# Shift and scale of attention in one adaLN block: a different split of the column sums between VectorE, ScalarE, GpSimd and TensorE

## The chip, the core and the metric

The kernel runs on one core of one Trainium2 chip. The metric is the device time of one execution in microseconds; the time given for a kernel is the median of several executions.

## The reference

One transformer block with adaptive layer norm, sequence 512, width 2048, all in float32. A conditioning vector `c` makes six vectors of 2048 numbers, and the first two of them, a shift and a scale, are applied to the normed input before one wide projection. Only this front part is touched by the change:

```python
sh_a, sc_a, g_a, sh_f, sc_f, g_f = jnp.split(jax.nn.silu(c) @ ada_w[l] + ada_b[l], 6, axis=-1)
h = rms_norm(x, norm_mix[l]) * (1.0 + sc_a[:, None, :]) + sh_a[:, None, :]
proj = h @ w_in[l]          # 2048 x 5656: convolution gates, q, k, v and gate logits
...                         # convolution mixer and sparse attention, out projection
x = x + g_a[:, None, :] * (y @ w_out[l])
h = modulate(rms_norm(x, norm_ffn[l]), sh_f, sc_f)
x = x + g_f[:, None, :] * ((jax.nn.silu(h @ ffn_w1[l]) * (h @ ffn_w3[l])) @ ffn_w2[l])
```

`ada_w` is 2048 x 12288. Shift and scale of attention are its first 4096 columns, 33.5 MB.

## The kernel before, in words

The kernel works through stages one after the other: the start stage (this change), the rest of q, k and v together with the compression of k and v, attention woven with the convolutions, the out projection, and the feed-forward part. Every product with a weight is done as three fp32r matmuls (`mm3`, L98 to L100) on operands split into a high and a low part; `load_split` (L85) loads a weight tile `raw` on SyncE's queue, casts the high part `whi` on ScalarE (L92) and subtracts on VectorE for the low part `wlo` (L93).

The **start stage** makes the input columns in steps. A column here is one block of 128 of the 2048 features, `k` from 0 to 15. Before the steps, x is loaded (4 MB), the row norms are taken, and four diagonal matrices `dg` are made from them (L270); TensorE turns x and scales it at once with 64 matmuls against `dg` (L278), which gives `xnT`, all 16 columns.

A step (`STEP = 2` columns, so eight steps) then has two parts, and `weave` puts the instructions of one part between those of the other, with 1.3 pieces of side work for each piece of main work:

- **side work** (`start_steps`): shift and scale of the *next* two columns. For scale and for shift apart (`m` = 1, 0), 256 columns of `ada_w` are loaded on SyncE's queue, four pieces of 512 KB, `ada_w` being laid so that each partition holds 16 rows. The 16 rows times `silu(c)` are added up per partition: 10 rows on VectorE (L187, L189), and 6 rows (`SHARE`) by ScalarE multiplying (L183) and GpSimd adding (L185); L192 adds the two sums. `ada_cols` then turns the sum `acc` on TensorE (L206) and VectorE sums over partitions (L208), which leaves 128 numbers per column in `shf` and `gsc`.
- **main work** (`start_columns`): `h` is `xnT` times scale plus shift on ScalarE (L293), split into `ahi` (L295) and `alo` (L296), and multiplied with `w_in`: 512 columns for k and v into `main` (24 matmuls), 128 for the gate logits (6), and, at fixed columns, 512 each for `ksv` and `q` in `aux`, which VectorE adds into SBUF (L322). All told 39 matmuls of 512 moving columns for each of the 16 columns, 624 in the stage. The first of a step needs `alo`, and with it shift and scale.

Each engine runs its instructions in the order in which they were put in its queue, so an instruction that waits holds what stands behind it on the same engine. The order printed below is that queue order.

Of the kernel before, what the change touches and what calls it, by code (L numbers as in the profile page):

```python
# [17 lines left out]
P = 128  # L18
D = 2048
S = 512  # L20
# [49 lines left out]
def block_kernel(ctx: ExitStack, tc: tile.TileContext, a: dict, out: bass.AP):  # L70
# [95 lines left out]
    def ada_steps(ring, width, c0, n, bias=False, second=None, share=0):  # L166


        acc = accp.tile([P, 512], F32, tag="acc", name="acc")[:, :n]
        acc2 = second.tile([P, 512], F32, tag="acc2", name="acc2", bufs=2)[:, :n] if share else None  # L170
        step = min(width // n, KC)
        yield acc
        if bias:
            nc.gpsimd.memset(acc, 0.0)
            nc.sync.dma_start(acc[0:1, :], a["ada_b"][:, c0:c0 + n])
        for k0 in range(0, KC, step):
            raw = ring.tile([P, width], F32, tag="araw", name="araw")
            rv = raw[:, :step * n].rearrange("p (k n) -> p k n", k=step)
            nc.sync.dma_start(rv, ada_v[:, k0:k0 + step, c0:c0 + n])
            for k in range(k0, k0 + step):  # L180
                w, s = rv[:, k - k0, :], cT[:, k:k + 1]
                if k < share:
                    nc.scalar.activation(w if k else acc2, w, AF.Copy, scale=s)  # L183
                    if k:
                        nc.gpsimd.tensor_add(acc2, acc2, w)  # L185
                elif k == share and not bias:
                    nc.vector.tensor_scalar(acc, w, s, None, op0=ALU.mult)  # L187
                else:
                    nc.vector.scalar_tensor_tensor(acc, w, s, acc, op0=ALU.mult, op1=ALU.add)  # L189
            yield  # L190
        if share:
            nc.vector.tensor_add(acc, acc, acc2)  # L192

    def ada(*args, **kw):
        steps = ada_steps(*args, **kw)
        acc = next(steps)
        for _ in steps:
            pass
        return acc
# [31 lines left out]
    aring = pool("araw", 4, stack=st0)  # L231
    STEP, AW, SHARE = 2, 1024, 6

    def start_steps(k0):

        if k0 < KC:
            for m in (1, 0):
                steps = ada_steps(aring, AW, m * D + k0 * P, STEP * P, second=sp, share=SHARE)
                acc = next(steps)
                yield from steps  # L240
                ada_cols(aux, acc, 0, m, k0, STEP)

    first = start_steps(0)
# [28 lines left out]
    for _ in range(KC * STEP * P // AW):  # L272
        next(first)
    xnT = []
    for k in range(KC):
        ps = aux()
        for i in range(NT):
            nc.tensor.matmul(ps[:, i * P:(i + 1) * P], xts[i][:, k * P:(k + 1) * P], dgs[i], start=True, stop=True)  # L278
        t = act.tile([P, S], F32, tag="alo", name="xnT")
        (nc.vector.tensor_copy if k % 4 == 3 else nc.scalar.copy)(t, ps)  # L280
        xnT.append(t)

# [3 lines left out]
    for _ in first:  # L286
        pass

    def start_columns(k0):
        n = STEP  # L290
# [17 lines left out]
        for c0, dst, ends in ((CKS, ksv, (0, 2, 4, 8, 12, 16)), (CQ, q0, (0, 2, 6, 10, 14, 16))):  # L308
# [3 lines left out]
            ws = [load_split(ring, rows(w_in, k, 2, c0, 512), 2, 512) for k in ks[::2]]  # L312
            for i in range(NT):
                ps = aux()
                tok = slice(i * P, (i + 1) * P)
                for k in ks:
                    mm3(ps, [h[:, tok] for h in hT[k]], [t[:, k % 2, :] for t in ws[(k - ks[0]) // 2]],
                        k == ks[0], k == ks[-1])
# [6 lines left out]
    for k0 in range(0, KC, STEP):  # L325
        weave(start_columns(k0), start_steps(k0 + STEP), 1.3)
# [834 lines left out]
```

## Time and profile before

| | |
|---|---|
| median of 3 runs | 2291.96 us (2291.7 to 2303.21) |
| the profiled execution | 2294.12 us, its span 2292.4 us |
| TensorE busy | 2220.5 us, 97% of the span |
| VectorE busy | 1684.2 us, 73% |
| ScalarE busy | 958.6 us, 42% |
| GpSimd busy | 132.0 us, 6% |
| start stage, first matmul with weights to the last | 44.57 to 219 us |

The times of single instructions come from one profiled execution. Busy times of TensorE overlap (matmuls are pipelined), so the time from the start of one matmul to the start of the next tells what one costs, not its duration. A row with two numbers of matmul records for one matmul is a plain fp32 matmul, which leaves two records; an fp32r matmul leaves one.

### The profile page before, as it was taken

How to read it: one execution, taken by the hardware profiler on the slowest of the kernel's cores; microseconds unless marked ns; L12 is line 12 of the kernel's file. 1: busy time of each engine (PE TensorE's matmuls, PEld its weight loads, DVE VectorE, ACT ScalarE, POOL GpSimd, SP SyncE). 2: the span in 40 equal slices, each digit the busy share in tenths (PEclk: the TensorE clock that was granted, in tenths of full speed). 3: DMA queues.
4: the chain of work that ended last, by engine and by line, in shares of the span. 5: the costliest groups of instructions: out<-in, count | busy, mean ns of one | idle time of the engine just before them, and what ended most of it. 6: DMA issues, size and time to landing. Idle time of an engine off the chain costs nothing.

```text
span 2292.4 us, 30011 instructions
## 1 busy us (share of the span) xinstructions
PE 2220.5 (97%) x11223; PEld 1856.7 (81%) x11223; DVE 1684.2 (73%) x2569; ACT 958.6 (42%) x1598; POOL 132.0 (6%) x205
## 2 busy tenths in 40 slices
PE   5889999999999999999999999999999999999999
PEld 4667777778787777788888888888888788888887
DVE  6996857877856773988888888888888655533356
ACT  6544434555444223744444444444444432222221
POOL 2430000000000000000000000000000200000010
PEclk9999999999999999999999999999999999999999
DMA  8785555545534873264333444434442675533243
GB/s 292 257 272 155 168 177 172 170 135 150 148 99 148 297 266 111 88 188 125 120 120 119 121 120 124 124 117 122 124 121 74 233 236 196 175 106 124 96 153 115
DMA packets 374406, 358.60 MB, mean 156 GB/s; under 512 B 14856, under 2 KB 288620, under 8 KB 373236
## 3 DMA queue, kind: packets, MB, share of 16 engines
q1 hardware_dynamic: 365364, 325.22, 45.3%
q0 software_dynamic: 8896, 31.46, 4.0%
q8 instruction: 88, 1.44, 0.3%
q14 instruction: 58, 0.48, 0.1%
HBM read 336.70 MB, written 19.92 MB: 156 GB/s over the span
## 4 chain that ended last, share of the span: by engine, by line
PE 45%; issue 36%; DVE 9%; DMA 7%; ACT 2%; POOL 1%; SPq 0%; POOLq 0%; DVEq 0%; ACTq 0%
PE main L98 8%; PE main L100 8%; PE main L99 8%; DMA araw<-in_ada_w 5%; DVE acc L189 4%; PE aux L98 4%; PE aux L100 4%; PE aux L99 4%; PE aux L676 2%; PE aux L648 1%; DVE wlo L93 1%; DMA raw<-in_w_in 1%; POOL gd L916 1%; PE aux L864 1%; PE main L864 1%
## 5 line engine op out<-in xcount | busy, mean ns | idle before, releaser
L92 ACT CAST whi<-raw 128x1024 fp32r<-128x1024 f32 (+1 forms) x168 | 171.6, 1021 | 464.9 <-PE main L100 268.6
L93 DVE TENSOR_TENSOR wlo<-raw,whi 128x1024 fp32r<-128x1024 f32 (+1 forms) x168 | 200.4, 1193 | 219.7 <-ACT whi L92 218.9
L864 PE MATMUL main<-hC,whi 128*128 128x512 f32 x1408 | 355.9, 394 | 5.5 <-DVE hC L881 3.3
L857 DVE TENSOR_TENSOR wlo<-raw,whi 128x1024 fp32r<-128x1024 f32 x218 | 265.8, 1220 | 107.4 <-ACT whi L852 107.4
L852 ACT CAST whi<-raw 128x1024 fp32r<-128x1024 f32 x218 | 228.2, 1047 | 259.3 <-PE main L864 129.1
L189 DVE SCALAR_TENSOR_TENSOR acc<-araw,cT,acc 128x512 f32<-128x512 f32 (+1 forms) x392 | 270.8, 692 | 79.0 <-DMA araw<-in_ada_w 69.2
L864 PEld LDWEIGHTS main<-hC,whi 128*128 128x128 f32 x1408 | 254.3, 190 | 52.1 <-DVE hC L881 4.4
L864 PE MATMUL aux<-hC,whi 128*128 128x512 f32 x1072 | 269.6, 393 | 0.0
L864 PEld LDWEIGHTS aux<-hC,whi 128*128 128x128 f32 x1072 | 193.7, 190 | 34.8
L866 PEld LDWEIGHTS main<-hC,wlo 128*128 128x128 f32 x1408 | 192.9, 191 | 13.9
L866 PE MATMUL main<-hC,wlo 128*128 128x256 f32 x1408 | 197.1, 283 | 0.0
L98 PE MATMUL main<-alo,whi 128*128 128x512 f32 x448 | 181.2, 405 | 11.3 <-DVE alo L296 11.3
L99 PE MATMUL main<-ahi,wlo 128*128 128x512 f32 x448 | 177.4, 396 | 0.0
L100 PE MATMUL main<-ahi,whi 128*128 128x512 f32 x448 | 177.1, 395 | 0.0
L866 PEld LDWEIGHTS aux<-hC,wlo 128*128 128x128 f32 x1072 | 146.4, 190 | 10.5
L98 PE MATMUL main<-wlo,ahi 128*128 128x512 f32 x384 | 152.1, 396 | 0.1
L100 PE MATMUL main<-whi,ahi 128*128 128x512 f32 x384 | 150.8, 393 | 0.0
L99 PE MATMUL main<-whi,alo 128*128 128x512 f32 x384 | 150.6, 392 | 0.0
L866 PE MATMUL aux<-hC,wlo 128*128 128x256 f32 x1072 | 149.8, 282 | 0.0
L852 ACT CAST whi<-t 128x1024 fp32r<-128x1024 f32 x84 | 88.3, 1051 | 136.5 <-PE aux L864 70.9
L98 PE MATMUL main<-wlo,ghi 128*128 128x512 f32 x352 | 138.3, 394 | 3.4 <-ACT ghi L1086 2.7
L98 PE MATMUL aux<-wlo,ghi 128*128 128x512 f32 x352 | 137.8, 391 | 0.0
(278 smaller groups left out, 3821.2 us busy)
## 6 DMA issues: line engine op xcount, KB each, us to landing
raw<-in_ffn_w SPq DMA_DIRECT2D x264, 512.0 KB
araw<-in_ada_w SPq DMA_DIRECT2D x136, 512.0 KB
araw<-in_ada_w SPq DMA_DIRECT2D x112, 256.0 KB
raw<-in_w_in SPq DMA_DIRECT2D x128, 192.0 KB
raw<-in_w_in SPq DMA_DIRECT2D x40, 512.0 KB
raw<-in_w_out SPq DMA_DIRECT2D x32, 512.0 KB
gd<-d POOLq DMA_DIRECT2D x44, 256.0 KB, 2.3
graw<-gd POOLq DMA_DIRECT2D x44, 256.0 KB, 4.2
```

The lines of the kernel that those rows point to most:

```text
L92: nc.scalar.copy(hi[:, :m], raw[:, :m])
L93: nc.vector.tensor_sub(lo[:, :m], raw[:, :m], hi[:, :m].bitcast(F32))
L98: nc.tensor.matmul(ps, lhs[0], rhs[1], start=first, stop=False)
L99: nc.tensor.matmul(ps, lhs[1], rhs[0], start=False, stop=False)
L100: nc.tensor.matmul(ps, lhs[0], rhs[0], start=False, stop=last)
L189: nc.vector.scalar_tensor_tensor(acc, w, s, acc, op0=ALU.mult, op1=ALU.add)
L648: nc.tensor.matmul(one[b], queries(g, i, h), kT[b][g][:, :L], start=True, stop=True)
L676: nc.tensor.matmul(po[:, b * HD:(b + 1) * HD], s["pT"][b][:, kb * P:(kb + 1) * P], vv[b][:, kb, g * HD:(g + 1) * HD], start=kb == 0, stop= ...
L852: nc.scalar.copy(hi, t)
L857: nc.vector.tensor_sub(lo, t, hi.bitcast(F32))
L864: nc.tensor.matmul(ps, wt[0][:, ks[k]], hC[p][:, k, :], start=first and k == 0, stop=False, skip_group_check=True)
L866: nc.tensor.matmul(ps[:, HS:], wt[1][:, ks[k]], hC[p][:, k, 0:HS], start=False, stop=last and k == HK - 1, skip_group_check=True)
```

## The change

- **Sums.** Shift and scale of a step are loaded side by side in one tile (`raw`, four `k` rows of 512 columns). VectorE adds up three of the four tiles (12 rows, L246 and L248 of the changed kernel) over both at once. The last tile goes to TensorE with the sum `acc`: for each block of 128 columns, `j`, 5 matmuls into partitions `32 j` to `32 j + 31` of one PSUM tile, with `crep` (`silu(c)` copied 32 times) or ones as the stationary operand of 32 columns (L254). ScalarE copies the result (`asb`, L258), one small matmul against a strided identity (L259) turns it, and VectorE adds the bias (L263) and makes the scale (L266). The shares of ScalarE and GpSimd (L183, L185, L192), the turns L206 and the sums L208 are gone.
- **Loads.** These loads are issued by GpSimd's queue (L241) in place of SyncE's, from a ring of three tiles of 1 MB in place of four of 512 KB.
- **x turned per step.** The matmuls against `dg` (L229 now) stand in `start_steps`, for the step's columns alone; all copies of `xnT` are ScalarE's.
- **Steps.** The first two steps have one column each (`PLAN`), then seven of two; the weave ratio is 0.7, and the blocks of `ksv` and `q` have an additional end after one column.

```diff
--- before.py
+++ after.py
@@ -163,13 +163,10 @@

     ada_v = ada_w.rearrange("(p k) n -> p k n", k=KC)

-    def ada_steps(ring, width, c0, n, bias=False, second=None, share=0):
+    def ada(ring, width, c0, n, bias=False):

         acc = accp.tile([P, 512], F32, tag="acc", name="acc")[:, :n]
-        acc2 = second.tile([P, 512], F32, tag="acc2", name="acc2", bufs=2)[:, :n] if share else None
         step = min(width // n, KC)
-        yield acc
         if bias:
             nc.gpsimd.memset(acc, 0.0)
             nc.sync.dma_start(acc[0:1, :], a["ada_b"][:, c0:c0 + n])
@@ -179,23 +176,10 @@
             nc.sync.dma_start(rv, ada_v[:, k0:k0 + step, c0:c0 + n])
             for k in range(k0, k0 + step):
                 w, s = rv[:, k - k0, :], cT[:, k:k + 1]
-                if k < share:
-                    nc.scalar.activation(w if k else acc2, w, AF.Copy, scale=s)
-                    if k:
-                        nc.gpsimd.tensor_add(acc2, acc2, w)
-                elif k == share and not bias:
+                if k == 0 and not bias:
                     nc.vector.tensor_scalar(acc, w, s, None, op0=ALU.mult)
                 else:
                     nc.vector.scalar_tensor_tensor(acc, w, s, acc, op0=ALU.mult, op1=ALU.add)
-            yield
-        if share:
-            nc.vector.tensor_add(acc, acc, acc2)
-    def ada(*args, **kw):
-        steps = ada_steps(*args, **kw)
-        acc = next(steps)
-        for _ in steps:
-            pass
         return acc

     def ada_cols(psum_tile, acc, which, m, k0, n):
@@ -228,19 +212,59 @@
     ksv = kp.tile([P, NT, 512], F32, name="ksv")
     q0 = kp.tile([P, NT, 512], F32, name="q0")
     raw_kv = kp.tile([P, 2, NKV, S], F32, name="raw_kv")
-    aring = pool("araw", 4, stack=st0)
-    STEP, AW, SHARE = 2, 1024, 6
-    def start_steps(k0):
-        if k0 < KC:
-            for m in (1, 0):
-                steps = ada_steps(aring, AW, m * D + k0 * P, STEP * P, second=sp, share=SHARE)
-                acc = next(steps)
-                yield from steps
-                ada_cols(aux, acc, 0, m, k0, STEP)
-    first = start_steps(0)
+    aring = pool("araw", 3, stack=st0)
+    PLAN = [(0, 1), (1, 1)] + [(k, 2) for k in range(2, KC, 2)]
+    AK = 4
+    crep = sp.tile([P, KC, 32], F32, name="crep")
+    nc.vector.tensor_copy(crep, cT[:, :, None].to_broadcast([P, KC, 32]))
+    xnT = []
+    def start_steps(k0, cn):
+        for k in range(k0, k0 + cn):
+            ps = aux()
+            for i in range(NT):
+                nc.tensor.matmul(ps[:, i * P:(i + 1) * P], xts[i][:, k * P:(k + 1) * P], dgs[i], start=True, stop=True)
+            t = act.tile([P, S], F32, tag="alo", name="xnT")
+            nc.scalar.copy(t, ps)
+            xnT.append(t)
+            yield
+        an, nq = cn * P, 2 * cn
+        acc = accp.tile([P, 512], F32, tag="acc", name="acc")[:, :nq * P]
+        raws = []
+        for k in range(0, KC, AK):
+            raw = aring.tile([P, AK, 512], F32, tag="araw", name="araw")
+            for m in range(2):
+                c0 = m * D + k0 * P
+                nc.gpsimd.dma_start(raw[:, :, m * an:(m + 1) * an], ada_v[:, k:k + AK, c0:c0 + an])
+            if k + AK < KC:
+                for kk in range(AK):
+                    w, s = raw[:, kk, :nq * P], cT[:, k + kk:k + kk + 1]
+                    if k + kk == 0:
+                        nc.vector.tensor_scalar(acc, w, s, None, op0=ALU.mult)
+                    else:
+                        nc.vector.scalar_tensor_tensor(acc, w, s, acc, op0=ALU.mult, op1=ALU.add)
+                yield
+        ps = aux()
+        for kk in range(AK + 1):
+            lhs, w = (crep[:, k + kk, :], raw[:, kk, :]) if kk < AK else (ones[:, 0:32], acc)
+            for j in range(nq):
+                nc.tensor.matmul(ps[32 * j:32 * j + 32, :P], lhs, w[:, j * P:(j + 1) * P], start=kk == 0, stop=kk == AK,
+                                 skip_group_check=True)
+        m = 32 * nq
+        asb = sp.tile([P, P], F32, tag="asb", name="asb", bufs=2)
+        nc.scalar.copy(asb[:m], ps[:m, :P])
+        nc.tensor.matmul(ps[:, 256:256 + nq], asb[:m], ident[:m, 0:m:32], start=True, stop=True, skip_group_check=True)
+        yield
+        for m, d in ((1, gsc), (0, shf)):
+            d = d[:, 0, k0:k0 + cn]
+            nc.vector.tensor_add(d, ps[:, 256 + m * cn:256 + (m + 1) * cn], bcol[:, m * KC + k0:m * KC + k0 + cn])
+            if m:
+                g0 = at["norm_mix"] + k0
+                nc.vector.scalar_tensor_tensor(d, d, 1.0, cols[:, g0:g0 + cn], op0=ALU.add, op1=ALU.mult)
     vrow = sp.tile([nrow, P], F32, name="vrow")
     brow = sp.tile([NB6, P], F32, name="brow")
     at, r0 = {}, 0
@@ -269,25 +293,13 @@
         dg = sp.tile([P, P], F32, name=f"dg{i}")
         nc.vector.tensor_scalar(dg, ident, ss, None, op0=ALU.mult)
         dgs.append(dg)
-    for _ in range(KC * STEP * P // AW):
-        next(first)
-    xnT = []
-    for k in range(KC):
-        ps = aux()
-        for i in range(NT):
-            nc.tensor.matmul(ps[:, i * P:(i + 1) * P], xts[i][:, k * P:(k + 1) * P], dgs[i], start=True, stop=True)
-        t = act.tile([P, S], F32, tag="alo", name="xnT")
-        (nc.vector.tensor_copy if k % 4 == 3 else nc.scalar.copy)(t, ps)
-        xnT.append(t)
     hT = []
     ps_kv = [main() for _ in range(4)]
     ps_gl = aux()
-    for _ in first:
+    for _ in start_steps(*PLAN[0]):
         pass

-    def start_columns(k0):
-        n = STEP
+    def start_columns(k0, n):
         for k in range(k0, k0 + n):
             h = sp.tile([P, S], F32, tag="h", name="h", bufs=2)
             nc.scalar.activation(h, xnT[k], AF.Identity, scale=gsc[:, 0, k:k + 1], bias=shf[:, 0, k:k + 1])
@@ -305,16 +317,17 @@
             mm3(ps_gl, [t[:, kk, :] for t in w], hT[k0 + kk], k0 + kk == 0, k0 + kk == KC - 1)
         yield

-        for c0, dst, ends in ((CKS, ksv, (0, 2, 4, 8, 12, 16)), (CQ, q0, (0, 2, 6, 10, 14, 16))):
+        for c0, dst, ends in ((CKS, ksv, (0, 1, 2, 4, 8, 12, 16)), (CQ, q0, (0, 1, 2, 6, 10, 14, 16))):
             if k0 + n not in ends:
                 continue
             ks = range(ends[ends.index(k0 + n) - 1], k0 + n)
-            ws = [load_split(ring, rows(w_in, k, 2, c0, 512), 2, 512) for k in ks[::2]]
+            m = min(len(ks), 2)
+            ws = [load_split(ring, rows(w_in, k, m, c0, 512), m, 512) for k in ks[::2]]
             for i in range(NT):
                 ps = aux()
                 tok = slice(i * P, (i + 1) * P)
                 for k in ks:
-                    mm3(ps, [h[:, tok] for h in hT[k]], [t[:, k % 2, :] for t in ws[(k - ks[0]) // 2]],
+                    mm3(ps, [h[:, tok] for h in hT[k]], [t[:, (k - ks[0]) % 2, :] for t in ws[(k - ks[0]) // 2]],
                         k == ks[0], k == ks[-1])
                 if k0 == 0:
                     nc.scalar.copy(dst[:, i, :], ps)
@@ -322,8 +335,8 @@
                     nc.vector.tensor_add(dst[:, i, :], ps, dst[:, i, :])
                 yield

-    for k0 in range(0, KC, STEP):
-        weave(start_columns(k0), start_steps(k0 + STEP), 1.3)
+    for i, step in enumerate(PLAN):
+        weave(start_columns(*step), start_steps(*PLAN[i + 1]) if i + 1 < len(PLAN) else iter(()), 0.7)
     for m in range(2):
         for g in range(NKV):
             (nc.vector.tensor_copy if g else nc.scalar.copy)(raw_kv[:, m, g, :], ps_kv[m * NKV + g])
```

VectorE's queue at the start of the program, before. `ss` is a row norm, `dg` the diagonal made from it, one for each quarter of the tokens; all four are needed for the first turn of x.

```order
L267 TENSOR_TENSOR ss_122<-sh_123 128x1
L124 RECIPROCAL ss_122<-ss_122 128x1
L267 TENSOR_TENSOR ss_133<-sh_134 128x1
L124 RECIPROCAL ss_133<-ss_133 128x1
L267 TENSOR_TENSOR ss_144<-sh_145 128x1
L124 RECIPROCAL ss_144<-ss_144 128x1
L270 TENSOR_SCALAR dg_131<-const,ss_122 128x128
L270 TENSOR_SCALAR dg_142<-const,ss_133 128x128
L270 TENSOR_SCALAR dg_153<-const,ss_144 128x128
L267 TENSOR_TENSOR ss_155<-sh_156 128x1
L124 RECIPROCAL ss_155<-ss_155 128x1
L270 TENSOR_SCALAR dg_164<-const,ss_155 128x128
```

The same place in the changed kernel, from the third norm on. Ahead of these rows stand the sums over three tiles of step 0 (L246 once, L248 eleven times), two more norms, and seven of the sums over the first two tiles of step 1.

```order
L124 RECIPROCAL ss_146<-ss_146 128x1
L248 SCALAR_TENSOR_TENSOR acc<-araw,cT,acc 128x256
L294 TENSOR_SCALAR dg_133<-const,ss_124 128x128
L294 TENSOR_SCALAR dg_144<-const,ss_135 128x128
L294 TENSOR_SCALAR dg_155<-const,ss_146 128x128
L248 SCALAR_TENSOR_TENSOR acc<-araw,cT,acc 128x256
L291 TENSOR_TENSOR ss_157<-sh_158 128x1
L248 SCALAR_TENSOR_TENSOR acc<-araw,cT,acc 128x256
L124 RECIPROCAL ss_157<-ss_157 128x1
L248 SCALAR_TENSOR_TENSOR acc<-araw,cT,acc 128x256
L294 TENSOR_SCALAR dg_166<-const,ss_157 128x128
```

Sums over `ada_w` tiles now stand between the norms; the first L248 of these rows is the last sum over step 1's second tile, and the last `dg` stands behind three sums over its third tile.

TensorE's queue at the end of a step in the steady part, before: the second turn of a sum (`acc`), and the first of the main matmuls behind it. Fifteen more like them follow, and then the next step's first row, `L98 MATMUL main`, which needs the shift.

```order
L206 MATMUL aux_1288<-const_87,acc_1204 128x128 x2
L98 MATMUL aux_1293<-wlo_1237,ahi_929 128x512
L99 MATMUL aux_1293<-whi_1236,alo_930 128x512
L100 MATMUL aux_1293<-whi_1236,ahi_929 128x512
L98 MATMUL aux_1293<-wlo_1237,ahi_935 128x512
L99 MATMUL aux_1293<-whi_1236,alo_936 128x512
L100 MATMUL aux_1293<-whi_1236,ahi_935 128x512
L98 MATMUL aux_1293<-wlo_1243,ahi_1126 128x512
L99 MATMUL aux_1293<-whi_1242,alo_1127 128x512
L100 MATMUL aux_1293<-whi_1242,ahi_1126 128x512
```

The same place in the changed kernel, for a step of two columns. Six main matmuls (L98 to L100 of `aux`) follow these rows, and then the next step's `L98 MATMUL main`.

```order
L254 MATMUL aux_1202<-araw_1199,crep_108 32x128 x16
L254 MATMUL aux_1202<-acc_1109,const_87 32x128 x4
L229 MATMUL aux_1259<-dg0_133,xt0_79 128x128
L229 MATMUL aux_1259<-dg1_144,xt1_81 128x128
L259 MATMUL aux_1202<-const_87,asb_1223 128x4
L229 MATMUL aux_1259<-dg2_155,xt2_83 128x128
L229 MATMUL aux_1259<-dg3_166,xt3_85 128x128
L229 MATMUL aux_1272<-dg0_133,xt0_79 128x128
L229 MATMUL aux_1272<-dg1_144,xt1_81 128x128
L229 MATMUL aux_1272<-dg2_155,xt2_83 128x128
L229 MATMUL aux_1272<-dg3_166,xt3_85 128x128
```

Between the matmul that ends shift and scale and the next step's first row stood 24 main matmuls; there now stand six turns of x and six main matmuls. The step's sum matmuls (20) and turns of x (8) are new in it, four turns L206 are gone.

## Rows read from the trace of the kernel before

**Rows 1.** The page's first part: busy time of each engine, share, instructions.

```profile
PE 2220.5 (97%) x11223; PEld 1856.7 (81%) x11223; DVE 1684.2 (73%) x2569; ACT 958.6 (42%) x1598; POOL 132.0 (6%) x205
```

**Rows 2.** Windows: length, busy time of each engine, PE clock, DMA share, GB/s.

```profile
0.00:44.57 44.57, 19.39 (x135) 18.54 (x135) 23.69 (x55) 30.48 (x60) 12.73 (x19) 0.93 0.80 276
44.57:219.40 174.83, 154.63 (x656) 121.89 (x656) 154.07 (x267) 90.06 (x167) 55.49 (x68) 0.97 0.74 244
219.40:345.00 125.60, 124.40 (x622) 94.65 (x622) 90.15 (x221) 51.21 (x141) 0.80 (x2) 1.00 0.54 167
```

**Rows 3.** Waits of TensorE, first 200 us: total, times, longest.

```profile
PE main L98 <- DVE alo L296: 11.3, 5, 6.7
PE aux L206 <- DVE acc L192: 7.9, 6, 2.8
PE aux L98 <- DVE wlo L93: 7.3, 4, 2.0
```

**Rows 4.** Timeline of TensorE: start, duration, instruction, count, idle before.

```profile
18.56 16.92 PE L278 MATMUL aux<-dg,xt 128*128 128x128 f32 x122 [1.03 <-DVE dg L270]
...
44.57 0.80 PE L98 MATMUL main<-alo,whi 128*128 128x512 f32 x1 [6.74 <-DVE alo L296]
...
131.28 0.50 PE L98 MATMUL main<-alo,whi 128*128 128x512 f32 x1 [0.48 <-DVE alo L296]
...
153.11 0.50 PE L98 MATMUL main<-alo,whi 128*128 128x512 f32 x1 [0.46 <-DVE alo L296]
...
195.85 0.39 PE L98 MATMUL main<-alo,whi 128*128 128x512 f32 x1
...
201.07 0.39 PE L100 MATMUL main<-ahi,whi 128*128 128x512 f32 x1
...
219.07 0.37 PE L334 MATMUL aux<-const,gl 32*128 32x32 f32 x3
```

**Rows 5.** Groups by form: count, busy, mean ns; the fourth from the whole execution.

```profile
L189 DVE SCALAR_TENSOR_TENSOR acc<-araw,cT,acc 128x256 f32<-128x256 f32 x144 | 84.9, 592 | 2.7 <-DMA araw<-in_ada_w 0.2
L187 DVE TENSOR_SCALAR acc<-araw,cT 128x256 f32<-128x256 f32 x16 | 11.4, 710 | 2.2 <-DMA araw<-in_ada_w 2.2
L192 DVE TENSOR_TENSOR acc<-acc,acc 128x256 f32<-128x256 f32 x16 | 9.8, 610 | 0.2
L189 DVE SCALAR_TENSOR_TENSOR acc<-araw,cT,acc 128x512 f32<-128x512 f32 x248 | 185.8, 750 | 76.3 <-DMA araw<-in_ada_w 69.0 <-DMA acc<-in_ada_b 3.6
L92 ACT CAST whi<-raw 128x256 fp32r<-128x256 f32 x8 | 3.2, 399 | 1.5 <-PE aux L100 0.8 <-DMA raw<-in_w_in 0.6
```

**Rows 6.** Timeline of TensorE in the compression stage, outputs in two partition halves.

```profile
264.49 0.38 PE L500 MATMUL aux<-ksv,blocks 128*62 128x256 f32 x1
264.49 0.38 PE L500 MATMUL aux<-raw,blocks 128*62 128x256 f32 x1
264.70 0.38 PE L500 MATMUL aux<-ksv,blocks 128*62 128x256 f32 x1
```

**Rows 7.** Transfers: windows of 10 us, and SyncE's queue in the first 200 us.

```profile
0.00:10.00 10.00, 0.00 (x0) 0.00 (x0) 0.22 (x2) 5.27 (x8) 0.20 (x4) 1.00 0.79 304
50.00:60.00 10.00, 7.20 (x33) 5.74 (x32) 9.01 (x18) 5.17 (x9) 1.91 (x3) 0.93 0.97 343
q1 hardware_dynamic: 43919, 52.45, 78.5%
```

**Rows 8.** Timelines of VectorE and ScalarE: a diagonal, and from shift to h.

```profile
18.22 0.29 DVE L270 TENSOR_SCALAR dg<-const,ss 128x128 f32<-128x128 f32 x1
...
150.10 0.16 DVE L210 TENSOR_TENSOR shf<-shf,bcol 128x2 f32<-128x2 f32 x1
...
150.30 1.52 ACT L293 ACTIVATE h<-xnT,shf,gsc 128x512 f32<-128x512 f32 x2 [4.88 <-DVE shf L210]
```

**Rows 9.** Line L806, 1 MB stores by GpSimd's queue: ns min/median/max, landing.

```profile
L806 POOL DMA_DIRECT2D xd<-x x4: 531/535/689, 769.7 to 916.4; - x4
...
DMA to landing us min/median/max: 5.1/5.3/5.9
```

## Prediction

> **What bounds the kernel now.** I read the shares first: TensorE is busy 97% of the span, VectorE 73% [rows 1], so only TensorE's idle time and its work can change the total. The windows by stage say where the idle time lies [rows 2]: 25.2 us before the first matmul with weights at 44.57 us, 20.2 us in the rest of the start stage (174.83 - 154.63), and then 1.2 us in the next 125.6. So the change is worth what it moves the end of the start stage; behind it TensorE is fed without a gap, and the stages there are the same. In the start stage VectorE is busy 154.07 of 174.83 us [rows 2], and the waits agree: TensorE waits for VectorE's `alo`, `acc` and `wlo` [rows 3]. Of the 11.3 us for `alo`, 6.7 are the first one, ahead of 44.57; 4.6 + 7.9 + 7.3 = 19.8 us are the 20.2 of the window.
>
> The timeline gives the units [rows 4]. One main matmul costs (201.07 - 195.85) / 23 = 0.227 us, 624 of them 141.6. The turn of x took 16.92 us for 122 records, 0.139 each, two records for a matmul. A full step in the steady part takes 153.11 - 131.28 = 21.8 us. The stage's last main matmul ends at 219.1, where the gate turns start. Sum of before from 44.57: 141.6 + 3.9 (28 turns L206 at 0.139) + 20.2 waits leaves 8.8 us of 174.5 unexplained; slow restarts after waits and a lower clock (mean 0.97 in this window [rows 2]) lie in it.
>
> **The change, part by part.**
>
> *VectorE.* Gone: 84.9 + 11.4 + 9.8 = 106.1 us [rows 5]. New: 77 sums of 512 columns at 750 ns, 57.8; 22 of 256 columns at 592, 13.0; nine first products at 710, 6.4; together 77 us. VectorE loses 29 us of its 154 and falls to about 70% of the stage. It stops being the bound, and TensorE's own queue becomes it.
>
> *Turns of x.* 64 matmuls, 17.8 us, stood at 18.56 to 35.5, while shift and scale of the first step were still being summed. In the new queue the turns of columns 0 and 1 stand ahead of the first main matmul; 14 columns come after it: 14 x 8 x 0.139 = 15.6 us that nothing hides, because TensorE is then the bound.
>
> *Column quarters on TensorE.* 160 matmuls of 128 moving columns, 10 of them before the first main matmul. Before has no four-quarter case. The nearest rows are the products with outputs in two partition halves [rows 6]: two start at the same time, and the next pair 0.21 us later, for 256 columns in one of two records. So 128 columns in one record cost 0.107 us, and halves run side by side. Bounds for the 150: four at a time 150 x 2 x 0.107 / 4 = 8.0 us; two at a time 16.1; one after the other at the turn's price, 150 x 2 x 0.139 = 41.7. Nearest are the halves, and quarters are the same thing in smaller pieces; I take 10, near to the four, with something for changes between the two kinds of matmul. The 28 turns L206 go (-3.9).
>
> *Start of the first step.* The last diagonal `dg` now stands behind sums over tile 7 of `ada_w` (tiles of 512 KB in the two one-column steps). All of x (4.2 MB), the constants (0.36 MB) and seven tiles (3.7 MB) must have landed: 8.2 MB at the 304 GB/s of the first 10 us [rows 7] gives 27.0 us, whichever queue is served first. The `dg` was made at 18.22 before [rows 8]. From there: `dg` 0.3, turn of one column 1.1, its 10 quarter matmuls 1.1 (at half clock), `asb` 0.4 (as the 256-column copy [rows 5]), its turn 0.3, and then the chain from shift to the first main matmul. That chain is 153.11 - 150.10 = 3.0 us from the addition L210 to TensorE [rows 4, 8]; with the scale's extra addition 0.15, the other addition 0.15 and half of a 750 ns sum in front of it on VectorE it makes 3.7. First main matmul at 27.0 + 6.9 = 33.9, against 44.57. Bounds: 343 GB/s, the best 10 us in the stage [rows 7], gives 31; if the first 1 MB tile of step 2 and the first weights, 1.9 MB, have to land first too, since two of its sums stand ahead of `alo` in VectorE's queue, 40.
>
> *End of each step.* L259 now waits for ScalarE's `asb` (0.4 us and the hand-overs), covered by two turns of x, 0.56. Behind L259 the next step's first main matmul needs the chain of 3.7 us. Its cover is six turns (1.67) and six main matmuls (1.36), 3.0; before, 24 matmuls (5.4 us) lay there and the wait was still 0.46 with VectorE's queue full [rows 4]. I take 0.7 us for each of the six transitions so ordered, 4.2 (bounds 0 and 1.5 each: 0 and 9). The waits for `acc` and `wlo`, 15.2 us [rows 3], shrink with VectorE's load: I take a fifth, 3.0 (bounds 0 and 8). Waits 7.2 in all. The unexplained 8.8 goes with the number of waits, and I take 5.
>
> *Loads.* From 44.57 on a step needs 4.2 MB of `ada_w` and 1.7 MB of `w_in`: 5.9 MB in 17.7 + 2.2 + 1.3 + 0.7 = 21.9 us (78 main matmuls, eight turns, quarter sums, wait), 269 GB/s. The queue gave 343 at a DMA share of 0.97, and the first 200 us moved 52.45 MB [rows 7]; so I cost the loads at nothing, with TensorE's work as cover. If that cover is gone, 52.45 MB at 304 GB/s end at 173 us, and the last step (102 matmuls, 23 us) still has to follow: 196 us, still less than the sum below.
>
> *Sum.* 33.9 + 141.6 + 15.6 + 10 + 7.2 + 5 = 213.3 us, against 219.1: 5.8 us less. Against the profiled execution's 2294.12 us that is 2288.3. It lies 2.16 us above the median of the runs shown, 2291.96, and from that the forecast is 2286.2 us.
>
> So the gains, 10.7 us at the start, 13.0 in waits and 3.8 in restarts, are mostly eaten by 15.6 us of turns and 10 - 3.9 of sums that TensorE now does while it is the bound. 0.5%, 11.5 us, is about what a measurement of this kernel can tell from no change.
>
> **The rivals.**
>
> *Faster: the covers hold.* First main matmul at 31, quarters at 8, waits 2, restarts 3: 31 + 141.6 + 15.6 + 8 + 2 + 3 = 201.2, 17.9 us less, 2274. For it: VectorE at 70% has slack, and halves run side by side [rows 6]. Against it: the chain behind L259 is longer than what stands there, and VectorE's queue is still served in order.
>
> *Slower: GpSimd's queue doesn't deliver.* A two-column step needs 4.2 MB through that queue in 21.9 us, 192 GB/s. The one large thing it moved before is a 1 MB store, landing after 5.3 us [rows 9], 198 GB/s with one transfer at a time and rows of 8 KB; the new loads have rows of 512 B and 1 KB, four to six in flight. Below 192 GB/s it decides; at 150 a step takes 28 us, seven times 6.1 more, 43 us, less the 5.8: 2329. For it: no row shows such a load, and a ring of three tiles has one tile held until TensorE's quarter sums. Against it: issuing the 1 MB took GpSimd only 0.53 us [rows 9], and more transfers overlap here.
>
> A one-source VectorE operation of 256 columns took 710 ns on the mean while GpSimd added, the two-source one 592 [rows 5]: something holds it. The Trainium skill, SBUF — State Buffer, section "SBUF: two separate sides", says that a DMA issued by GpSimd can't have its descriptors written while VectorE runs a two-port operation (fp32 copies and one-source products within SBUF), and it advises the other queues. By that rule the nine first products would hold the queue for nine times 0.7 us, one in each step; that alone would not bring it to 150 GB/s, so by it the forecast would stand.
>
> *Slower: the quarters run one after the other.* 41.7 in place of 10: 31.7 us more, less the 5.8: 2318. Against it stand the halves [rows 6].
>
> **How the numbers follow.** Forecast (the end of the stage moves by less than 11.5 us): 0.51. Covers hold, about 2274: 0.28. GpSimd's queue too slow, about 2329 or more: 0.13. Quarters in series, 2318: 0.04. All upper bounds together, start 33.9 to 40, waits 7.2 to 17, quarters 10 to 16, 21.9 us more less the 5.8, 2308: 0.04. So faster 0.28, same 0.51, slower 0.21. The forecast's own range is 2279 to 2301, from its bounds of start and waits. The range of 8 in 10 reaches to the faster case and to the last one: 2272 to 2311, leaving out the two dear cases and the best part of the faster one.
>
> **What would show it.** First main matmul near 34 us; TensorE's turns of x spread over the stage with 2.2 us a step; the quarter sums starting four together, 20 within 1.1 to 2 us; waits for `alo` below 1 us a step and few for `acc`; VectorE near 70% in the stage; the last main matmul near 213. The prediction is wrong if the load of a tile lands more than about 10 us after its issue in the steady part (queue), if quarter sums start one by one 0.1 us or more apart (series), or if the first main matmul is past 40 us.

## The result, and the profile after

The changed kernel takes 2309.38 us (median of 9 runs, 2304.04 to 2316.8) against 2295.86 before (9 runs): a ratio of 1.0062, 95% interval 1.0047 to 1.0077 (both as recorded; the quotient of the two medians is 1.0059). The forecast was 2286.2, so the direction was wrong. The profiled execution has a span of 2305.5 us, 13.1 more than before, and the place where they come in is the start stage: its last main matmul ends, and the gate turns follow, at 230.09 us in place of 219.07, 11.0 later. The other 2.1 us come behind the stage.

Windows of the changed kernel: ahead of the first main matmul, from it to the gate turns, and a stretch behind (columns as in [rows 2]).

```profile
0.00:39.93 39.93, 7.34 (x41) 5.57 (x41) 17.14 (x50) 16.81 (x31) 15.20 (x24) 0.97 0.83 309
39.93:230.10 190.17, 175.41 (x1053) 139.74 (x1053) 128.81 (x199) 68.71 (x114) 39.78 (x55) 0.99 0.65 223
230.10:392.00 161.90, 159.83 (x801) 123.62 (x800) 116.69 (x284) 66.41 (x180) 0.63 (x2) 1.00 0.55 169
```

Against [rows 2]: the first main matmul comes 4.6 us sooner, VectorE falls from 154.07 of 174.83 us to 128.81 of 190.17, 68%, and TensorE is busy 175.41 us where it was 154.63. Behind the stage TensorE runs as before.

TensorE's waits from the first main matmul to the gate turns (that matmul's own 4.3 us are in the first row):

```profile
PE main L98 <- DVE alo L308: 9.7, 8, 4.3
PE aux L98 <- DVE wlo L93: 7.0, 5, 2.1
PE aux L98 <- DVE gsc L266: 0.9, 1, 0.9
PE aux L229 <- DVE ksv L335: 0.6, 1, 0.6
PE aux L259 <- ACT asb L258: 0.4, 1, 0.4
PE aux L98 <- DVE ksv L335: 0.3, 1, 0.3
```

Against [rows 3] the waits for `acc` are gone, and those for `wlo`, 7.3 before, are not.

I added up TensorE's timeline from start to start, with the idle time ahead of an instruction taken out, and it gives the forecast's sum term by term:

| us | forecast | measured |
|---|---|---|
| first main matmul | 33.9 | 39.93 |
| main matmuls with restarts and low clock | 141.6 + 5 | 150.27 |
| turns of x | 15.6 | 13.82 |
| quarter sums, and the small turn L259 | 10 | 9.95 + 1.57 |
| waits | 7.2 | 14.54 |
| gate turns | 213.3 | 230.09 |

Before, the same count gives 44.57 + 152.26 (main) + 2.27 (L206) + 19.97 (waits) + 0.29 up to the row behind. So TensorE took on 13.82 + 11.52 - 2.27 = 23.1 us of work and got back 4.6 at the start, 2.0 in main matmuls and 5.4 of waits.

**What the waits are made of.** First the chain of one of them: rows of VectorE's timeline, then of ScalarE's, GpSimd's and TensorE's; then what the view of line L241 says of the last of the four issues that start at 108.73 (who waited for it, and its time to landing), and two windows (columns as in [rows 2]).

```profile
114.83 0.75 DVE L248 SCALAR_TENSOR_TENSOR acc<-araw,cT,acc 128x512 f32<-128x512 f32 x1
119.58 0.49 DVE L246 TENSOR_SCALAR acc<-araw,cT 128x512 f32<-128x512 f32 x1 [4.00 <-DMA araw<-in_ada_w]
120.11 3.11 DVE L248 SCALAR_TENSOR_TENSOR acc<-araw,cT,acc 128x512 f32<-128x512 f32 x4
123.14 2.35 DVE L93 TENSOR_TENSOR wlo<-raw,whi 128x1024 fp32r<-128x1024 f32 x2
```
```profile
120.14 1.06 ACT L92 CAST whi<-raw 128x1024 fp32r<-128x1024 f32 x1 [5.12 <-PE main L100]
```
```profile
108.73 2.97 POOL L241 DMA_DIRECT2D araw<-in_ada_w  x4 [2.14 <-DVE acc L248]
```
```profile
124.41 0.50 PE L98 MATMUL aux<-wlo,ahi 128*128 128x512 f32 x1 [1.36 <-DVE wlo L93]
```
```profile
  DVE acc L246: 4.0, 1
...
DMA to landing us min/median/max: 8.5/8.5/8.5
```
```profile
112.00:120.00 8.00, 7.32 (x34) 5.75 (x33) 3.92 (x7) 3.02 (x6) 1.49 (x2) 1.00 0.95 347
120.00:123.00 3.00, 3.00 (x14) 2.19 (x12) 2.86 (x5) 2.11 (x2) 0.27 (x1) 1.00 0.28 113
```

VectorE stands idle for 4.00 us in front of a sum whose tile was asked for by the last two of four loads in a row, begun when an earlier tile came free. The last of them took 8.5 us to land, the DMA engines being busy to 0.95 meanwhile; right behind it they are busy to 0.28. VectorE then works off five sums, and `wlo`, whose input was ready at 121.20, starts at 123.14. An engine with a third of its time free makes TensorE wait, because a sum that waits for a load stands ahead. From 45 to 170 us VectorE waits 13.5 + 4.0 = 17.5 us for loads:

```profile
DVE acc L246 <- DMA araw<-in_ada_w: 13.5, 6, 4.3
DVE acc L248 <- DMA araw<-in_ada_w: 4.0, 2, 2.2
```

The start is late by the same pattern. VectorE's rows ahead of the first main matmul:

```profile
28.66 0.48 DVE L248 SCALAR_TENSOR_TENSOR acc<-araw,cT,acc 128x256 f32<-128x256 f32 x1 [0.90 <-DMA araw<-in_ada_w]
...
30.10 0.28 DVE L294 TENSOR_SCALAR dg<-const,ss 128x128 f32<-128x128 f32 x1
...
35.20 0.16 DVE L266 SCALAR_TENSOR_TENSOR gsc<-gsc,cols 128x1 f32<-128x1 f32 x1
38.00 0.49 DVE L246 TENSOR_SCALAR acc<-araw,cT 128x512 f32<-128x512 f32 x1 [2.64 <-DMA araw<-in_ada_w]
38.52 0.75 DVE L248 SCALAR_TENSOR_TENSOR acc<-araw,cT,acc 128x512 f32<-128x512 f32 x1
39.19 0.69 DVE L308 TENSOR_TENSOR alo<-h,ahi 128x512 fp32r<-128x512 f32 x1
```

The last diagonal is made at 30.10 (18.22 before, [rows 8]), and `alo` stands behind a sum that waits 2.64 us for the next step's tile.

### The profile page after: what moved, and what is told of

It reads as the page before. It is cut to its first block, busy times and chain, and to the rows that moved or that the text cites. A ratio compares the mean times of both kernels' runs of the same rounds, so it can differ in the third digit from the quotient of the medians.

```text
span 2305.5 us, 30300 instructions
## 1 busy us (share of the span) xinstructions
PE 2229.2 (97%) x11529; PEld 1861.1 (81%) x11529; DVE 1653.1 (72%) x2497; ACT 924.0 (40%) x1519; POOL 118.0 (5%) x197
## 4 chain that ended last, share of the span: by engine, by line
PE 41%; issue 35%; DMA 11%; DVE 9%; POOL 2%; ACT 1%; SPq 0%; DVEq 0%; POOLq 0%; ACTq 0%
DMA araw<-in_ada_w 9%; PE main L98 7%; PE main L99 7%; PE main L100 7%; PE aux L98 4%; PE aux L100 4%; PE aux L99 4%; DVE acc L182 2%; DVE acc L248 1%; PE aux L689 1%; DVE wlo L93 1%; DMA raw<-in_w_in 1%; POOL gd L929 1%; DMA graw<-gd 1%; PE main L877 1%
## 5 line engine op out<-in xcount | busy, mean ns | idle before, releaser
L92 ACT CAST whi<-raw 128x1024 fp32r<-128x1024 f32 (+2 forms) x172 | 172.5, 1003 | 524.0 <-PE main L100 304.5
L93 DVE TENSOR_TENSOR wlo<-raw,whi 128x1024 fp32r<-128x1024 f32 (+2 forms) x172 | 199.2, 1161 | 228.9 <-ACT whi L92 228.2
L182 DVE SCALAR_TENSOR_TENSOR acc<-araw,cT,acc 128x512 f32<-128x512 f32 x248 | 185.9, 750 | 76.8 <-DMA araw<-in_ada_w 69.3
L98 PE MATMUL main<-alo,whi 128*128 128x512 f32 x448 | 181.1, 404 | 10.0 <-DVE alo L308 9.7
L100 PE MATMUL main<-ahi,whi 128*128 128x512 f32 x448 | 176.7, 394 | 0.0
L98 PE MATMUL main<-wlo,ahi 128*128 128x512 f32 x384 | 152.0, 396 | 1.6 <-DVE t L816 1.5
L100 PE MATMUL main<-whi,ahi 128*128 128x512 f32 x384 | 150.8, 393 | 0.0
L98 PE MATMUL main<-wlo,ghi 128*128 128x512 f32 x352 | 138.2, 394 | 3.2 <-ACT ghi L1099 2.8
L98 PE MATMUL aux<-wlo,ghi 128*128 128x512 f32 x352 | 137.8, 391 | 0.0
```

Of the source, the lines that this page charges most:

```text
L92: nc.scalar.copy(hi[:, :m], raw[:, :m])
L93: nc.vector.tensor_sub(lo[:, :m], raw[:, :m], hi[:, :m].bitcast(F32))
L98: nc.tensor.matmul(ps, lhs[0], rhs[1], start=first, stop=False)
L100: nc.tensor.matmul(ps, lhs[0], rhs[0], start=False, stop=last)
```

## The experiments

Gate turns, first main matmul and waits are of one profile each; the ratio, with its 95% interval, is as recorded, to runs of the kernel before that go with each kernel's own (medians 2295.86 to 2296.64). Behind the gate turns 2072 to 2077 us of span are left (2080 in the two fastest), so the gate turns tell what the stage does.

| kernel | first main | gate turns | waits between | median us, ratio |
|---|---|---|---|---|
| before | 44.57 | 219.07 | 20.0 | 2295.86 |
| changed | 39.93 | 230.09 | 14.5 | 2309.38, 1.0062 [1.0047, 1.0077] |
| x up front | 52.77 | 227.15 | 10.3 | 2305.47, 1.0048 [1.0033, 1.0064] |
| SyncE loads | 31.93 | 218.63 | 9.9 | 2296.09, 0.9995 [0.9984, 1.0007] |
| six half tiles | 40.00 | 234.35 | 16.8 | 2311.53, 1.0069 [1.0050, 1.0089] |
| norms first | 35.36 | 227.61 | 15.0 | 2304.58, 1.0040 [1.0025, 1.0056] |
| GpSimd loads, SyncE's order | 36.35 | 220.77 | 9.0 | 2298.79, 1.0010 [1.0000, 1.0021] |
| SyncE loads, changed order | 44.58 | 232.65 | 12.5 | 2311.34, 1.0069 [1.0052, 1.0086] |
| SyncE loads, x up front | 39.75 | 206.62 | 4.9 | 2288.31, 0.9961 [0.9948, 0.9974] |
| before, x per step | 40.16 | 226.80 | 21.1 | 2304.32, 1.0042 [1.0027, 1.0056] |
| parts ahead of sums | 40.44 | 237.41 | 14.7 | 2314.88, 1.0080 [1.0065, 1.0095] |
| fourteen rows | 38.63 | 206.42 | 8.1 | 2288.08, 0.9962 [0.9950, 0.9973] |
| all rows on VectorE | 39.96 | 223.42 | 24.2 | 2301.24, 1.0031 [1.0019, 1.0042] |

**x up front.** The turns leave `start_steps` and stand ahead of the first step.

```diff
...
+    for k in range(KC):
+        ps = aux()
+        for i in range(NT):
+            nc.tensor.matmul(ps[:, i * P:(i + 1) * P], xts[i][:, k * P:(k + 1) * P], dgs[i], start=True, stop=True)
+        t = act.tile([P, S], F32, tag="alo", name="xnT")
+        nc.scalar.copy(t, ps)
+        xnT.append(t)
     hT = []
```

> The changed kernel, but x turned as before: all 64 matmuls against the diagonals ahead of the first step. Changed kernel: first main matmul 39.9 us, last one 229.8. Theory A (in the start stage TensorE pays for its own added work; its waits come from VectorE's queue): the 13.8 us of turns and 1.6 us of waits for them leave the steps, but stand ahead of the first main matmul, which moves from 39.9 to about 52 (last diagonal at 30.4, 15 more columns at 1.1 us, then quarter sums and the chain). Last main matmul about 227, time about 3 us less than the changed kernel. Rival B (turns only filled waits): the waits in the steps grow by what the turns leave, and the last main matmul comes at 240 or later.

Measured 52.77 and 227.15, as theory A has it. The steps shrink by 190.2 - 174.4 = 15.8 us, the turns and a part of the waits with them: turns don't fill waits.

**SyncE loads, six half tiles, norms first.** One edit each to the changed kernel:

```diff
-                nc.gpsimd.dma_start(raw[:, :, m * an:(m + 1) * an], ada_v[:, k:k + AK, c0:c0 + an])
+                nc.sync.dma_start(raw[:, :, m * an:(m + 1) * an], ada_v[:, k:k + AK, c0:c0 + an])
```
```diff
-    aring = pool("araw", 3, stack=st0)
+    aring = pool("araw", 6, stack=st0)
-    AK = 4
+    AK = 2
...
```
```diff
...
+    with tc.issue_after(last_dg.ins):
+        for _ in start_steps(*PLAN[0]):
+            pass
```

> The changed kernel, but the loads of ada_w on SyncE's queue, as before. They then stand behind x, so the norms come ahead of the sums on VectorE, and in the steps each load stands behind the weights' loads. Theory A (a load is late because its tile came free late): the landing time in the steps stays near the 5.5 us of the changed kernel and the waits for alo and wlo in the steps, 9.9 us, stay between 8 and 14; first main matmul near 35, last one near 226. Rival C (GpSimd's queue delivers slowly): landing falls below 4 us, the waits fall to 5 or less, last main matmul 220 or earlier.

> The changed kernel, with the same ring memory cut finer: six tiles of 512 KB with two rows each, in place of three tiles of 1 MB with four rows. A tile comes free after two sums in place of four. Theory A (VectorE waits for loads that were issued only when it had freed a tile, and alo and wlo stand behind those sums): VectorE's waits for loads in the steps, about 17 us from 58 to 170, fall by half, TensorE's waits for alo and wlo, 9.9 us, fall to about 5, the last main matmul comes at about 225. Rival D (the loads are limited by bandwidth, not by when a tile is free): nothing moves by more than 2 us, last main matmul 228 to 232.

> The changed kernel, but on VectorE all sums over ada_w stand behind the last diagonal. Theory A (diagonals were late because sums that wait for loads stood ahead of them): last diagonal at 18 to 20 us in place of 30.1, first main matmul at about 34, last one about 224, time about 6 us less than the changed kernel. Rival E (the sums take the time that the diagonals save, since the loads can't come earlier): first main matmul 38 to 41, last one 228 to 231, same time.

SyncE's loads bring the gate turns 11.5 us sooner, as far as rival C asked for, but not by its reason: a load takes no less from issue to landing (median 5.8 us against 5.5). The waits for `alo` and `wlo` from 58 to 170 us, 6.5 where the changed kernel has 10.0, lie between the two forecasts, and 8.0 of the 11.5 us come at the start. The finer tiles miss both forecasts, 4.3 us later, though VectorE's waits for loads from 45 to 170 us fall to 12.2. GpSimd takes about as long to issue a small load as a large one (722 and 748 ns) and is busy 58.59 us of 110 with 82 of them, where it was 31.63 with 43; that this is the cause is not shown, since the order of VectorE's instructions changed as well. Norms first gives back 4.6 us at the start, of the 5.9 forecast, but the steps are 192.3 us long, 2.1 more than in the changed kernel, so the start alone doesn't explain it.

**Queue or order?** The kernel's instructions are put in order when it is built, and the traces show that the one-line edit to the loads' queue also moved VectorE's instructions (norms ahead of sums, and other places for sums among `alo`, `wlo` and L335) and some of TensorE's and ScalarE's. Two kernels cross the two: each keeps one queue for the loads, and takes the order of VectorE, ScalarE and TensorE in the start stage from the other (lines stand 7 further down in them).

```diff
+    by = {i.name: i for i in nc.cur_bb.bb.instructions}
+    for queue in ORDER:
...
+        for one, other in zip(names, names[1:]):
+            tc.add_manual_dep(by[other], one, mybir.DependencyInfo(mybir.DependencyClass.NoSync, mybir.DependencyReason.DATA),
+                              reason="order")
```

> The changed kernel, loads on GpSimd's queue, but in the start stage the instructions of VectorE, ScalarE and TensorE stand in the order that the kernel with loads on SyncE's queue had. Gate turns of the start stage: 230.1 us in the changed kernel, 218.6 with SyncE's loads. Theory O (the moved loads cost because the order on VectorE came out otherwise: sums that wait for a load stand ahead of the norms, alo and wlo): gate turns at 219 to 223. Rival Q (the queue itself delivers a tile later after it is free): gate turns at 227 to 231.

> The counterpart: loads on SyncE's queue, but in the start stage the instructions of VectorE, ScalarE and TensorE stand in the changed kernel's order. Theory O: gate turns at 227 to 231, or later at the start, since the sums ahead of the norms then wait for loads that stand behind x. Rival Q: gate turns at 219 to 223, and VectorE's waits for loads from 45 to 170 us at half the changed kernel's 17 us.

Order decides. With GpSimd's loads the other order is worth 230.09 - 220.77 = 9.3 us, with SyncE's 232.65 - 218.63 = 14.0; the queue, at one order, 2.1 one way and 2.6 the other. Rival Q falls. Behind the 2.1 and 2.6 lie two opposite parts: with the other's order, either queue has its first main matmul 4.4 or 4.7 us later and its steps 2.3 or 2.1 us shorter. TensorE's largest waits from 30 us on and VectorE's for loads from 45 to 170 us, in the kernel with GpSimd's loads and SyncE's order:

```profile
PE main L105 <- DVE alo L315: 9.3, 7, 3.7
PE aux L105 <- DVE wlo L100: 2.5, 3, 1.3
```
```profile
DVE acc L253 <- DMA araw<-in_ada_w: 4.4, 2, 4.0
DVE acc L255 <- DMA araw<-in_ada_w: 3.1, 2, 2.1
```

VectorE now waits 7.5 us for loads from the same queue and ring, in place of 17.5. The counterpart shows the start at its worst: with x ahead of the loads on one queue, a sum that stands first waits 15.31 us, and all norms behind it.

```profile
18.37 0.35 DVE L253 TENSOR_SCALAR acc<-araw,cT 128x256 f32<-128x256 f32 x1 [15.31 <-DMA araw<-in_ada_w]
```

**Parts ahead of sums.** The changed kernel in its own order, with 27 rows moved.

> The changed kernel with its own order kept on VectorE, ScalarE and TensorE through the start stage, but for one thing: on VectorE, behind the first alo, each wlo moves ahead of up to three and each alo ahead of up to two sums (L246, L248) that stand right before it (27 of 48 move). Start unchanged: first main matmul at 39.9. Theory O' (in the steps TensorE waits because alo and wlo stand behind sums): waits for wlo fall from 7.0 to 2 us or less, those for alo in the steps from 5.4 to about 4.5, gate turns at 223 to 226 in place of 230.1. Rival (the sums that now come later hold the quarter sums and the loads, and a wait for them takes its place): gate turns at 228 to 232, with new waits at the quarter sums.

The theory in this form falls, and the rival too, in size (237.41) and in the place of the new waits. The waits for `wlo` are nearly gone, and others stand in their place. VectorE's rows and TensorE's of one:

```profile
109.46 1.54 DVE L255 SCALAR_TENSOR_TENSOR acc<-araw,cT,acc 128x512 f32<-128x512 f32 x2 [3.21 <-DMA araw<-in_ada_w]
110.92 0.68 DVE L342 TENSOR_TENSOR q<-aux,q 128x512 f32<-128x512 f32 x1
```
```profile
111.66 0.71 PE L236 MATMUL aux<-dg,xt 128*128 128x128 f32 x4 [2.15 <-DVE q L342]
112.20 0.28 PE L266 MATMUL aux<-const,asb 128*128 128x4 f32 x2
112.35 0.69 PE L236 MATMUL aux<-dg,xt 128*128 128x128 f32 x4
114.04 2.07 PE L236 MATMUL aux<-dg,xt 128*128 128x128 f32 x8 [1.00 <-DVE q L342]
```

It is the same stall with another victim: a sum waits 3.21 us for its load, and what stands behind it now is the addition that frees TensorE's PSUM buffer. In all the waits are as long as before the move (14.7 us); 6.6 of the 7.3 us more are main matmuls and turns that took longer, and the lower clock shown in the last section is enough for them: three stretches of 17.0 us in all at half the clock.

**What the parts are worth.** The kernel before with x turned per step, and the changed kernel with SyncE's loads and x up front (the first and the second diff above together; the one-column steps, the ring of 1 MB tiles and the weave ratio of the change are still in it):

> The kernel before, with one part of the change alone: x turned per step. Before: first main matmul 44.6 us, gate turns 219.1, 20.0 us of waits between. Theory A: first main matmul at 40 to 44; 15.6 us of turns go into the steps, where they fill at most half of the waits for acc and wlo; gate turns at 221 to 227, time 2 to 8 us more. Rival B (turns only fill waits): gate turns at 219 or earlier, waits in the steps 5 us or less.

> The changed kernel with loads on SyncE's queue and x turned up front, as before: only the sums and their column quarters are left of the change. Theory A (turns in the steps are added work of TensorE, while ahead of the first step TensorE waits anyway): first main matmul at 40 to 43 us in place of 31.9, 14.4 us of turns less behind it, gate turns at 209 to 214, time 2284 to 2290 us. Rival B (turns only filled waits): waits in the steps grow, gate turns at 217 or later, time about 2295 us.

Both came out by theory A, the second better than it: 4.9 us of waits are left, and from 85 to 185 us TensorE is busy without a gap. VectorE's waits for loads from 45 to 170 us, 17.5 in the changed kernel, are 0.7 here.

```profile
DVE acc L240 <- DMA araw<-in_ada_w: 0.7, 1, 0.7
```
```profile
85.00:185.00 100.00, 100.00 (x605) 80.52 (x604) 78.67 (x123) 32.00 (x46) 1.07 (x3) 0.98 0.81 273
39.75:206.60 166.85, 161.86 (x940) 127.64 (x940) 128.66 (x201) 62.14 (x100) 1.07 (x3) 0.98 0.79 262
```

This version beats both kernels, 0.9961 [0.9948, 0.9974]. Half of its 12.4 us is given back behind the stage (span less gate turns: 2079.9 against 2073.3); where that is lost stays open.

**How many rows for TensorE.** From that version, VectorE takes 14 rows (with the six half tiles above, the last of them for TensorE), or all 16, with TensorE's quarters for the sum alone (the diff is that of the latter):

```diff
-            if k + AK < KC:
+            if True:
...
-        for kk in range(AK + 1):
...
+        for j in range(nq):
+            nc.tensor.matmul(ps[32 * j:32 * j + 32, :P], ones[:, 0:32], acc[:, j * P:(j + 1) * P], start=True, stop=True,
+                             skip_group_check=True)
```

> The kernel with loads on SyncE's queue and x turned up front (gate turns 206.6, 2288.3 us), but VectorE sums 14 of the 16 rows and TensorE's quarters take two rows and the sum, from six tiles of 512 KB. Theory A (TensorE is the bound there, VectorE has room): the quarter sums fall from 10.6 to about 6.5 us, gate turns at 202 to 205. Rival (VectorE's queue fills again, by 1.5 us in each step): waits for wlo and alo take it back, gate turns at 206 to 210.

> The same kernel (loads on SyncE's queue, x turned up front), but VectorE sums all 16 rows, and TensorE's column quarters take only the sum. TensorE does about 7.8 us less, VectorE some 25 us more: 128.7 + 25 = 154 us between the first main matmul and the gate turns. Theory A (the share that TensorE took is worth its price only as long as VectorE would be full otherwise): waits for alo and wlo grow by 5 to 10 us, gate turns at 204 to 210, no better than the 206.6 of the kernel with quarters. Rival (VectorE's slack takes them all): gate turns at 201 or earlier.

14 rows change nothing that can be measured, as the rival has it: the quarter sums fall to 7.3 us, and the waits grow from 4.9 to 8.1. With all 16 the waits are 24.2 us and the gate turns at 223.42, past both forecasts:

```profile
PE main L98 <- DVE alo L305: 20.1, 9, 4.4
PE aux L244 <- DVE acc L240: 8.2, 1, 8.2
```

So the four rows that TensorE takes, 7.8 us of its time (the quarters of the sum stay), are worth 223.42 - 206.62 = 16.8 us net of that. The order of the instructions is another one in these two kernels as well, and was not held.

## Why the prediction was wrong

The step that failed is "It stops being the bound, and TensorE's own queue becomes it", with its companion "I cost the loads at nothing". VectorE's share was forecast well (about 70%, measured 68%), but a share says nothing of the order in which a queue is served: VectorE is free for a third of the time, and yet TensorE waited 14.54 us, nearly all of it for VectorE, where 7.2 were forecast. Sums that wait for loads stood ahead of `alo`, `wlo` and the norms, and with another order of the same instructions the gate turns come 9.3 us sooner, 3.6 of them at the start and 5.7 in the steps. The stage's miss, 230.09 - 213.3 = 16.8 us, is 6.0 at the start, 7.3 in waits, 3.7 in main matmuls and 1.6 for the small turn, less 1.8 at the turns of x. The measured 2309.38 lies within the wide range, 2272 to 2311, next to the case with all upper bounds together (2308, chance 0.04). That nearness is partly luck: start and waits did come near their bounds, but the quarters stayed at 10, and restarts and small turn, which that case leaves as they were, make up 5.3 us. Point by point:

- **Loads at nothing: wrong.** The mean rate was there, 278 GB/s in the steps from 60 to 170 us where 269 was the need, and still VectorE waited 17.5 us. A load starts only when a tile is free, so the loads come in bursts, and those that VectorE waited for took 4.9 to 8.6 us to land. The bound that I set was one of mean rate, and the price was one of latency in front of an engine served in order.
- **Waits 7.2: measured 14.54.** Those for `alo` behind the first, 5.4, were near the 4.2 forecast. Those for `wlo` did not shrink with VectorE's load. The crossed kernels show 9.0 with the same edits in another order.
- **First main matmul 33.9: measured 39.93.** I took the time by which 8.2 MB land at 304 GB/s, 27.0, for the last diagonal, which came at 30.10. The loads were faster (417 GB/s from 5 to 15 us); what was late was the chain between VectorE and ScalarE through the norms, with sums that wait for loads in between. The upper bound, 40, named the other half: sums of step 2 ahead of `alo`. With the norms first it is 35.36.
- **Turns of x 15.6: right** (13.82). What they cost on balance, a sooner start set against them, is another matter: 7.7 us in the kernel before, 2.9 in the changed kernel, 12.0 with SyncE's loads.
- **Quarters 10: right** (9.95), four side by side. What I left out is the small turn, 1.57.
- **Restarts 5: measured 8.7** (150.27 - 141.6). Before, the same count gives 10.7 (152.26 - 141.6) and not 8.8, since the 28 turns L206, priced at 3.9, take 2.27. So this term fell by 2.0 us, with waits 5.4 us shorter, where 3.8 was forecast.
- **The rival that GpSimd's queue doesn't deliver** is out: 2 to 3 us by the crossed kernels. (The 1 MB store was not the one large thing that queue had moved: the page of before also lists 44 loads `graw<-gd` of 256 KB by it, landing in 4.2 us.) The Trainium skill, SBUF — State Buffer, section "SBUF: two separate sides", has a DMA issued by GpSimd held while VectorE runs a two-port operation. No row here shows that: the 72 issues in the stage took 747 to 888 ns, median 748, and landed in a median of 5.5 us. But only four of them overlap a copy or a one-source product of VectorE within SBUF, so this case hardly tests it.

Taken apart by the experiments, in gate turns: sums and quarters with x up front and SyncE's loads 206.62 - 219.07 = -12.4 us, x turned per step +12.0 (to 218.63), the order that came with GpSimd's loads and that queue +11.5 (to 230.09). These are the prices along one path, and they don't simply add: with x up front, GpSimd's loads and their order cost 227.15 - 206.62 = 20.5, and x per step then only 2.9. Not settled is which rows of that order, on VectorE or the other two engines, cost the 5.7 us in the steps (190.2 against 184.4; 5.5 are waits); moving `alo` and `wlo` alone was not it.

## What to carry to other kernels

A wait for a load that stands in the queue of a shared engine holds everything behind it, so a share of 68% need not be slack; look at what each waiting row has behind it. Where instructions are put in order at build time, an edit to a DMA's queue is also an edit to the order on every engine: compare the orders first, and cross order and edit to tell them apart. Work that moves from inside a stage into idle time ahead of it is cheaper there, but not free: x up front moved the first main matmul back by 7.8 us with SyncE's loads and shortened the steps by 19.8; in the changed kernel it was 12.8 against 15.8.

## What the runs showed of the hardware

- Four column quarters run side by side: 32 records of 128 columns start within 0.90 us, 0.028 each, where a turn of 128 columns costs 0.139 a record [rows 4] (0.123 in the changed kernel's steps, 13.82 / 112).

```profile
203.82 1.08 PE L254 MATMUL aux<-araw,crep 128*32 128x128 f32 x32
204.72 0.40 PE L254 MATMUL aux<-acc,const 128*32 128x128 f32 x8
```

- Issuing a load costs GpSimd a median of 748 ns, whether it is of 256 or of 512 KB; on SyncE the same loads took a median of 480.
- TensorE's clock, in the kernel with parts ahead of sums: granted 1.00 to 112.2 us, then, behind the waits of 2.15 and 1.00 us shown above, 0.50 (1.2 of 2.4 GHz) from 114.0 to 118.5, and a main matmul costs 0.43 us in place of 0.23. The same level is granted again from 140.4 to 147.2, behind waits of 2.17 and 1.00 us, and from 171.1 to 174.5, behind one of 2.36. In the changed kernel a wait of 2.11 us at 148.45 left it at 1.00. The mean over that stage was 0.95 against 0.99, and main matmuls with turns took 6.6 us more: nearly all of what that kernel lost.

```profile
109.10:112.20 3.10, 0.95 (x20) 0.68 (x13) 2.70 (x5) 0.53 (x2) 1.49 (x2) 1.00 0.94 342
112.20:114.00 1.80, 0.84 (x8) 0.65 (x6) 1.76 (x4) 0.00 (x0) 0.32 (x1) 0.75 1.01 410
114.00:118.50 4.50, 4.46 (x15) 3.79 (x16) 3.08 (x7) 3.08 (x6) 1.17 (x2) 0.50 0.86 291
```
